# Keeping the two parts of each split weight tile in DRAM

## The chip, the cores and the metric

The kernel runs on one core of one Trainium2 chip. The metric is the device time of one launch in microseconds: the median of three runs.

## The reference

One inference step of a two-layer decoder trunk, for a prompt of 2048 tokens and a sample group of 8 sequences with one new token and 2048 past tokens each (width 1024, all in float32). Both groups share the weights.

```python
def even_mixer(x, past_kv, w_in, w_sp, b_sp):          # layer 0
    h = einsum('btd,de->bte', x, w_in)                 # 1024 x 3584
    u, v, gate_a, q, k, vb, gate_b = split(h)
    out_a = chunk_spatial_gate(gelu(u), standardize(gelu(v))) * silu(gate_a)
    out_b = stick_breaking(q, keys, vals) * silu(gate_b)
    return concat([out_a, out_b])

def odd_mixer(x, ...):                                 # layer 1
    h = einsum('btd,de->bte', x, w_in)                 # 1024 x 2468
    q, kv, q_idx, k_idx, w_idx, gate_c, p, gate_d = split(h)
    out_c = dsa_attend(top 256 keys by the index scores) * silu(gate_c)
    out_d = multiscale_pool(p) * silu(gate_d)
    return concat([out_c, out_d])

x = layer_norm(alpha * x + mixer(x) @ w_out[layer])    # 1024 x 1024, after each mixer
```

The outputs are both groups' results and the new entries of the caches.

## The kernel before, in words

The prompt is cut into four blocks of 512 tokens. For each block there is an input projection of layer 0 (`p0`, 28 weight tiles of 1024 x 128), an output projection of layer 0 (`out_proj` with `out0`, 8 weight tiles of 512 x 256), two parts of the input projection of layer 1 (`p1a`, 8 tiles, one of them only 36 columns wide; `p1b`, 12 tiles) and an output projection of layer 1 (`out1`, 8 tiles). Every block goes through the same weights, so each tile is used four times; the last block's `out1` is done in two parts, and its tail takes four of the tiles a second time (lines 1823 to 1835).

All these products are made to nearly full float32 precision on TensorE by splitting both operands in two parts of 12 bits each, hi + lo = the value, and adding three products (`proj`, lines 165 to 167; `out_proj`, lines 560 to 562). A weight tile is split anew each time it is used, in `load_w` (lines 86 to 95): a transfer brings the raw tile from the input (line 89: 512 KB, in rows of 512 B for the input projections and of 1 KB for the output projections), ScalarE casts it to hi (line 91), and GpSimd and VectorE each subtract one half for lo (line 94). The raw tiles have two buffers (tag `wr`), hi and lo two each (tags `wh`, `wl`; 4 KB of each partition per buffer). There are 260 such loads: 112 of layer 0's input weights, 80 of layer 1's and 68 of the output weights.

The order of the weights is written out as a list of stages (`plan_w`, line 243). Two tiles are loaded ahead; then each `proj` takes one tile from the list `wready` and at its end starts the load of a later one (`more_w`, line 262). `out_proj` takes two tiles at once, the two halves of the contraction for 256 columns, goes over the four token tiles in two pairs, and calls `more_w` when the last token tile of the second pair is done with a half.

The work is traced by generators. `par` (line 1837) runs several streams side by side, each at its share of an estimated cost, and the framework then orders the instructions of each engine by a simulated time line with the traced order as priority. The stages (lines 1782 to 1835) come in three contexts, each with its own pools of SBUF:

- first context: `p0(0)` alone with the sample group's columns; then `p0(1)`, `o0(0)` with `p0(2)`, and `p1a(0)`, `p1b(0)`, `o0(1)`, `p0(3)`, each beside mixer B of the block before and the sample group's attention over its cached pages (`sample0`, a third stream);
- second context: `o0(2)`, `p1a(1)`, `p1b(1)`, `p1a(2)`, `p1b(2)` beside mixer C's first tiles, with the rest of mixer B in the third stream;
- third context: `o0(3)`, `p1a(3)`, `p1b(3)` and the output projections of layer 1 beside mixer C's later tiles and the sample group's layer 1.

All ordinary transfers are issued by SyncE's one queue: raw weights, the parts of q, k and v (`qsc`, `ksc`, `vsc`), which go through DRAM and come back for each step of mixer B, the sample group's pages (`pg`), and so on. A transfer that waits for a buffer holds up those issued after it.

The functions that the change touches are these.

Of the kernel before, what the change touches and what calls it, by code (L numbers as in the profile page):

```python
# [19 lines left out]
P = 128  # L20
D = 1024
# [14 lines left out]
BUFS = {"tmp": 4, "tok": 4, "ot": 3, "hl": 1, "wr": 2}  # L36
# [18 lines left out]
class Body:  # L55
    def __init__(self, ctx, tc, I, O):
# [7 lines left out]
        self.wp = pool("wp", 2)  # L64
# [3 lines left out]
    # ---------------------------------------------------------------- helpers  # L68
# [5 lines left out]
    def split(self, hi, lo, src, heng, leng):  # L74
        """hi + lo = src exactly, hi and lo of 12 bits each"""
# [10 lines left out]
    def load_w(self, src, shape, pool, bufs=2):  # L86
        nc = self.nc
        raw = self.loc.tile(shape, F32, tag="wr", name="wr", bufs=self.bufs["wr"])
        nc.sync.dma_start(raw, src)
        hi, lo = (pool.tile(shape, F32R, tag=n, name=n, bufs=bufs) for n in ("wh", "wl"))  # L90
        nc.scalar.copy(hi, raw)  # L91
        h = shape[1] // 2
        for e, c in ((nc.gpsimd, slice(0, h)), (nc.vector, slice(h, 2 * h))):
            e.tensor_tensor(lo[:, c], raw[:, c], hi[:, c].bitcast(F32), op=OP.subtract)  # L94
        return hi, lo

    def rsqrt(self, out, var, eps, n):
        """out = (var + eps) ** -0.5, [n, k] in SBUF"""
# [14 lines left out]
    def ps(self, name, shape=(P, TB)):  # L113
        """a PSUM bank, of the first of its pools that the phase has"""
# [12 lines left out]
    # ---------------------------------------------------------------- tokens  # L127
    def load_xT(self, src, after=False, lag=0):
        """512 tokens, channels on partitions, in two parts; after: of rows that are still to be normalized"""
# [46 lines left out]
    def sample_proj(self, smp, w, m, c0):  # L176
        """the sample group's columns: [16, m] = parts of x by tokens, then summed with channels on partitions"""
# [18 lines left out]
    # ---------------------------------------------------------------- layer 0  # L196
    def setup0(self):
# [17 lines left out]
        # scratch  # L215
# [10 lines left out]
    def pools(self, bufs, navb=0, navc=0, width=0):  # L226
        """the pools of a phase; its mixer C takes tiles of up to width keys"""
# [15 lines left out]
    def plan_w(self, stages):  # L243
        """the weights that the stages take, in their order; two tiles are loaded ahead"""
        I = self.I
        self.wplan, self.wready = [], []
        for st in stages:
            if st[:3] == "out":
                w = I["w_out"][int(st[3])]
                self.wplan += [(w[hf * 512:(hf + 1) * 512, cg * 256:(cg + 1) * 256], [P, 4, 256])  # L250
                               for cg in range(4) for hf in HALVES[int(st[3])]]
                continue
# [5 lines left out]
            self.wplan += [(w[:, c:c + n], [P, KT, n]) for c, n in cols]  # L258
        for _ in range(2):
            self.more_w()  # L260

    def more_w(self, pool=None):
        if self.wplan:
            src, shape = self.wplan.pop(0)
            src = src.rearrange("(kt p) n -> p kt n", p=P)
            self.wready.append(self.load_w(src, shape, *((pool, 4) if pool else (self.wp,))))

    def gelu2(self, ps, out):
        """2 gelu(ps) to out (SBUF)"""
# [16 lines left out]
    def p0(self, i, smp=None):  # L286
        """projections of block i, mixer A, and what mixer B needs"""
# [13 lines left out]
        # q  # L301
# [7 lines left out]
        # k  # L309
# [19 lines left out]
        # v: its channels on partitions, with the token before the block in column 0  # L329
# [27 lines left out]
        # mixer A  # L357
# [14 lines left out]
        # gate of B  # L372
# [34 lines left out]
    def weave(self, a, b):  # L407
        """two generators in turns; the value of the first, which yields None while it needs the second to go on"""
# [30 lines left out]
    def b_logits(self, i, step, prev):  # L439
        """1 - sigmoid of the logits of four query tiles to one block of keys, as a product from the last key on"""  # L440
# [35 lines left out]
    def b_values(self, i, step, Ps):  # L476
        """the products, transposed, times the differences of the values"""
# [1416 lines left out]
```

## Time and profile before

| | |
|---|---|
| median of three runs | 3286.61 us (3285.94 to 3306.84) |
| profiled execution, span | 3300.5 us |
| profiled execution, mean granted clock of TensorE | 0.933 |
| TensorE busy (matmul) | 2941.0 us, 89% |
| VectorE busy | 2363.4 us, 72% |
| ScalarE busy | 1592.6 us, 48% |
| GpSimd busy | 1100.1 us, 33% |
| moved by DMA | 536.68 MB, 163 GB/s over the span |

The profile is of one execution; its own time is the span from the first to the last instruction, 3300.5 us, 13.9 us above the median of the runs. PE is TensorE's matmuls, PEld its weight loads, DVE VectorE, ACT ScalarE, POOL GpSimd, SP SyncE. A group's row gives line, engine, operation, what it writes and reads, its count, then busy microseconds and mean nanoseconds of one, then the engine's idle time just before it and who ended it. In a table of stretches come start and end, length, the busy time of each engine with its instructions in brackets, and last the granted clock as a share of full speed, the share of the 16 DMA engines that was busy, and GB/s.

### The profile page before, as it was taken

How to read it: one execution, taken by the hardware profiler on the slowest of the kernel's cores; microseconds unless marked ns; L12 is line 12 of the kernel's file. 1: busy time of each engine (PE TensorE's matmuls, PEld its weight loads, DVE VectorE, ACT ScalarE, POOL GpSimd, SP SyncE). 2: the span in 40 equal slices, each digit the busy share in tenths (PEclk: the TensorE clock that was granted, in tenths of full speed). 3: DMA queues.
4: the chain of work that ended last, by engine and by line, in shares of the span. 5: the costliest groups of instructions: out<-in, count | busy, mean ns of one | idle time of the engine just before them, and what ended most of it. 6: DMA issues, size and time to landing. Idle time of an engine off the chain costs nothing. (4 is left out here: it accounts for less than half of the span.)

```text
span 3300.5 us, 53011 instructions
## 1 busy us (share of the span) xinstructions
PE 2941.0 (89%) x17490; PEld 2339.4 (71%) x17490; DVE 2363.4 (72%) x5797; ACT 1592.6 (48%) x3212; POOL 1100.1 (33%) x1188
## 2 busy tenths in 40 slices
PE   8996999999899888998798898897979899989897
PEld 6774776777678667787576566665857778878676
DVE  2255477776876787669868988786798677697845
ACT  3332434244334233444345666565566567557653
POOL 2231334432324333242322312224322344444422
PEclk9997999999899999999799899998979999989898
DMA  7436767786575667454564344333555455657542
GB/s 224 125 108 158 235 194 217 233 239 177 173 220 151 205 207 227 144 169 120 158 172 114 111 132 127 98 92 91 154 175 140 131 170 160 196 171 211 181 130 66
DMA packets 543391, 536.68 MB, mean 163 GB/s; under 512 B 43831, under 2 KB 408528, under 8 KB 543079
## 3 DMA queue, kind: packets, MB, share of 16 engines
q1 hardware_dynamic: 533231, 497.39, 51.9%
q0 software_dynamic: 9856, 35.66, 3.5%
q8 instruction: 139, 2.28, 0.3%
q14 instruction: 165, 1.35, 0.1%
HBM read 439.19 MB, written 93.92 MB: 162 GB/s over the span
## 5 line engine op out<-in xcount | busy, mean ns | idle before, releaser
L94 POOL TENSOR_TENSOR wl<-wr,wh 128x512 fp32r<-128x512 f32 x260 | 413.4, 1591 | 945.0 <-ACT wh L91 844.8
L165 PE MATMUL pp<-xh,wh 128*128 128x512 f32 x1536 | 625.2, 412 | 18.7 <-DVE q_hl L84 5.3
L166 PE MATMUL pp<-xl,wh 128*128 128x512 f32 x1536 | 621.5, 405 | 14.6 <-DVE xl L84 9.8
L167 PE MATMUL pp<-xh,wl 128*128 128x512 f32 x1536 | 618.3, 403 | 1.9 <-POOL wl L94 1.9
L91 ACT CAST wh<-wr 128x1024 fp32r<-128x1024 f32 x260 | 269.9, 1039 | 338.7 <-PE pp L166 135.3
L471 DVE TENSOR_TENSOR_SCAN P<-P 128x512 f32<-128x512 f32 (+2 forms) x320 | 380.3, 1201 | 53.9 <-ACT P L464 25.3
L165 PEld LDWEIGHTS pp<-xh,wh 128*128 128x128 f32 x1536 | 293.3, 192 | 96.2 <-issue 11.4
L166 PEld LDWEIGHTS pp<-xl,wh 128*128 128x128 f32 x1536 | 294.1, 192 | 74.6 <-DVE xl L84 16.2
L94 DVE TENSOR_TENSOR wl<-wr,wh 128x512 fp32r<-128x512 f32 x260 | 226.8, 873 | 163.3 <-ACT wh L91 154.3
L167 PEld LDWEIGHTS pp<-xh,wl 128*128 128x128 f32 x1536 | 293.2, 191 | 65.3 <-POOL wl L94 4.4
L560 PE MATMUL pp_o<-wh,oh 128*128 128x256 f32 x1008 | 297.1, 299 | 18.9 <-DVE xres L565 9.1
L561 PE MATMUL pp_o<-wl,oh 128*128 128x256 f32 x1008 | 292.5, 293 | 1.2 <-POOL wl L94 1.1
L562 PE MATMUL pp_o<-wh,ol 128*128 128x256 f32 x1008 | 288.8, 294 | 0.9 <-POOL ol L84 0.7
L1194 PE MATMUL z_c<-ksc,qc 128*128 128x512 f32 (+3 forms) x816 | 226.4, 370 | 48.9 <-DVE mx L1196 41.6
L1212 ACT ACTIVATE zt<-zt,nmax 128x512 f32<-128x512 f32 (+3 forms) x320 | 207.4, 651 | 118.9 <-DVE nmax L1200 118.7
L1181 POOL TENSOR_TENSOR nm<-nm,mk 128x256 f32<-128x256 f32 (+1 forms) x128 | 95.0, 743 | 449.6 <-DMA nm<-bft 293.3
L78 ACT CAST ph<-ps_p 128x512 fp32r<-128x512 f32 (+1 forms) x320 | 164.5, 524 | 165.9 <-PE ps_p L490 156.5
L84 DVE TENSOR_TENSOR pl<-ps_p,ph 128x512 fp32r<-128x512 f32 (+1 forms) x320 | 189.4, 598 | 74.4 <-ACT ph L78 73.7
L457 PE MATMUL z<-ks,q 128*128 128x512 f32 (+3 forms) x640 | 199.3, 402 | 38.3 <-DVE mx L1196 23.4
L1239 PE MATMUL av_c<-zt,vsc 128*64 128x128 f32 x2176 | 216.9, 301 | 16.5 <-ACT zt L1227 16.3
L1227 ACT COPY zt<-ps_pc 128x512 f32<-128x512 f32 (+3 forms) x320 | 162.8, 518 | 135.1 <-PE ps_pc L1225 131.6
L940 ACT ACTIVATE mk<-ix,tk_tn 128x384 int8<-128x384 f32 (+13 forms) x140 | 183.5, 1310 | 86.5 <-DVE tk_tn L990 46.2
(460 smaller groups left out, 6311.0 us busy)
## 6 DMA issues: line engine op xcount, KB each, us to landing
pg<-cache_b_kv SPq DMA_DIRECT2D x256, 256.0 KB
wr<-w_in_even SPq DMA_DIRECT2D x112, 512.0 KB
wr<-w_in_odd SPq DMA_DIRECT2D x76, 512.0 KB
wr<-w_out SPq DMA_DIRECT2D x68, 512.0 KB
ks<-ksc SPq DMA_DIRECT2D x80, 256.0 KB
vs<-vsc SPq DMA_DIRECT2D x80, 256.0 KB
ksc<-kcs SPq DMA_DIRECT2D x80, 256.0 KB
q<-qsc SPq DMA_DIRECT2D x64, 256.0 KB
```

Of the source, the lines that this page charges most:

```text
L91: nc.scalar.copy(hi, raw)
L94: e.tensor_tensor(lo[:, c], raw[:, c], hi[:, c].bitcast(F32), op=OP.subtract)
L165: nc.tensor.matmul(ps[:m], wh[:, kt, :m], xh[kt], start=a, stop=False)
L166: nc.tensor.matmul(ps[:m], wh[:, kt, :m], xl[kt], start=False, stop=False)
L167: nc.tensor.matmul(ps[:m], wl[:, kt, :m], xh[kt], start=False, stop=b)
L471: nc.vector.tensor_tensor_scan(r, r, r, initial=ini, op0=OP.mult, op1=OP.bypass)
L560: nc.tensor.matmul(ps[:, :256], oh[:, tt], wh[:, k], start=a, stop=False)
L561: nc.tensor.matmul(ps[:, :256], oh[:, tt], wl[:, k], start=False, stop=False)
L562: nc.tensor.matmul(ps[:, :256], ol[:, tt], wh[:, k], start=False, stop=b)
L1194: nc.tensor.matmul(z[:, :n], q2[:, c, jj % 2, :].bitcast(F32R), kk, start=c == 0, stop=c == 1)
L1212: nc.scalar.activation(zt, zt, AF.Exp, bias=nmx, accum_out=st["rs"][:, h, c:c + 1])
L1239: nc.tensor.matmul(self.av[64 * a:64 * a + 64, g, jj // 2, :], vs[:, k, :], pT[:, k * P:(k + 1) * P], start=kb == 0, stop=kb == nkb - 1)
```

## The change

A weight tile's two parts now lie side by side in one tile `w2` (8 KB of each partition, three buffers). The first time a tile is used it is loaded raw and split as before, and then both parts are written to a scratch tensor in DRAM, 1 MB, 8 KB in a row for each partition. Each later use reads this tensor back in one transfer straight into `w2`, with no cast and no subtraction. A key (stage and column, or layer, column group and half) tells whether a tile has been kept.

The raw tiles' two buffers are in a pool of the first context alone. So that layer 1's output weights, whose first use is later, are split by then too, `split_ahead(1)` takes its 8 tiles through split and write at the end of the third stream of the first context's last stage. There are 64 different tiles; so 64 raw loads with their splits, 64 writes and 204 reads take the place of 260 raw loads with their splits.

```diff
-BUFS = {"tmp": 4, "tok": 4, "ot": 3, "hl": 1, "wr": 2}
+BUFS = {"tmp": 4, "tok": 4, "ot": 3, "hl": 1}
...
-        self.wp = pool("wp", 2)
+        self.wp = pool("wp", 3)
+        self.wkept = {}
...
-    def load_w(self, src, shape, pool, bufs=2):
+    def load_w(self, key, src, shape, pool, bufs):
         nc = self.nc
-        raw = self.loc.tile(shape, F32, tag="wr", name="wr", bufs=self.bufs["wr"])
+        w2 = pool.tile([P, 2, shape[1] * shape[2]], F32R, tag="w2", name="w2", bufs=bufs)
+        hi, lo = (w2[:, c].rearrange("p (k n) -> p k n", k=shape[1]) for c in range(2))
+        if key in self.wkept:
+            nc.sync.dma_start(w2.bitcast(F32), self.wkept[key])
+            return hi, lo
+        raw = self.wraw.tile(shape, F32, tag="wr", name="wr", bufs=2)
         nc.sync.dma_start(raw, src)
-        hi, lo = (pool.tile(shape, F32R, tag=n, name=n, bufs=bufs) for n in ("wh", "wl"))
         nc.scalar.copy(hi, raw)
         h = shape[1] // 2
         for e, c in ((nc.gpsimd, slice(0, h)), (nc.vector, slice(h, 2 * h))):
             e.tensor_tensor(lo[:, c], raw[:, c], hi[:, c].bitcast(F32), op=OP.subtract)
+        d = self.wkept[key] = self.dr.tile([P, 2, shape[1] * shape[2]], F32, name=f"wk{len(self.wkept)}")
+        nc.sync.dma_start(d, w2.bitcast(F32))
         return hi, lo
...
-            self.wplan += [(w[:, c:c + n], [P, KT, n]) for c, n in cols]
+            self.wplan += [((st[:2], c), w[:, c:c + n], [P, KT, n]) for c, n in cols]
...
+    def out_w(self, layer):
+        w = self.I["w_out"][layer]
+        return [((f"out{layer}", cg, hf), w[hf * 512:(hf + 1) * 512, cg * 256:(cg + 1) * 256], [P, 4, 256])
+                for cg in range(4) for hf in HALVES[layer]]
+
+    def take_w(self, key, src, shape, pool, bufs):
+        return self.load_w(key, src.rearrange("(kt p) n -> p kt n", p=P), shape, pool, bufs)
+
     def more_w(self, pool=None):
         if self.wplan:
-            src, shape = self.wplan.pop(0)
-            src = src.rearrange("(kt p) n -> p kt n", p=P)
-            self.wready.append(self.load_w(src, shape, *((pool, 4) if pool else (self.wp,))))
+            self.wready.append(self.take_w(*self.wplan.pop(0), pool or self.wp, 4 if pool else 3))
+
+    def split_ahead(self, layer):
+        for w in self.out_w(layer):
+            self.take_w(*w, self.wp, 3)
+            yield 1.0
...
             self.pools(BUFS_A, navb=1)
+            self.wraw = self.cx.enter_context(self.tc.tile_pool(name="wraw", bufs=2))
...
-            self.par([(p1a(0), PB), (p1b(0), PC), (o0(1), PO), (p0(3), PA)], [(mb(2), B(2))], [(until(bg, 1000), S0[2])], early=EARLY[0])
+            self.par([(p1a(0), PB), (p1b(0), PC), (o0(1), PO), (p0(3), PA)], [(mb(2), B(2))], [(until(bg, 1000), S0[2]), (self.split_ahead(1), 8)], early=EARLY[0])
```

More of the change, by code (lines that the diff above doesn't have):

```diff
@@ L248, in plan_w @@
             if st[:3] == "out":
-                w = I["w_out"][int(st[3])]
-                self.wplan += [(w[hf * 512:(hf + 1) * 512, cg * 256:(cg + 1) * 256], [P, 4, 256])
-                               for cg in range(4) for hf in HALVES[int(st[3])]]
+                self.wplan += self.out_w(int(st[3]))
                 continue
```

## The prediction

> **What bounds the kernel now.** I read the page's busy times first, then the span cut into the three phases that the code has (0 to 300 us: block 0 alone; 300 to 1450 us: layer 0 beside mixer B and the sample group; 1450 to 3300 us: mostly layer 1), and then the idle time of TensorE (PE).
>
> ```profile
> span 3300.5 us, 53011 instructions
> PE 2941.0 (89%) x17490; PEld 2339.4 (71%) x17490; DVE 2363.4 (72%) x5797; ACT 1592.6 (48%) x3212; POOL 1100.1 (33%) x1188
> DMA packets 543391, 536.68 MB, mean 163 GB/s; under 512 B 43831, under 2 KB 408528, under 8 KB 543079
> ```
>
> ```profile
> 0.00:300.00 300.00, 251.12 (x1458) 202.18 (x1459) 103.61 (x268) 92.59 (x179) 71.14 (x70) 0.93 0.52 142
> 300.00:1450.00 1150.00, 1066.53 (x5338) 821.46 (x5336) 816.00 (x1280) 437.09 (x824) 395.32 (x423) 0.96 0.67 202
> 1450.00:3300.00 1850.00, 1623.38 (x10696) 1315.76 (x10696) 1443.76 (x4250) 1062.97 (x2211) 633.62 (x697) 0.92 0.49 142
> ```
>
> The columns after the length are PE, PEld, DVE, ACT and POOL busy, then the granted clock of PE, the share of the 16 DMA engines and GB/s. PE is the bound with 89%, but not a full one: it idles 83.5 us in the middle phase (1150 - 1066.5) and 226.6 us in the late one (1850 - 1623.4), and where it idles its clock is lower too: 0.96 and 0.92. At 0.92 the late phase's 1623 us hold some 130 us of lost speed, so beside each idle microsecond stands 0.57 us of slow clock (130 / 226.6); in the middle phase 0.04 x 1066.5 / 83.5 = 0.51.
>
> What ends PE's idle time are above all answers of VectorE (DVE), not weights (us in total, times, longest):
>
> ```profile
> PE z_c L1194 <- DVE mx L1196: 41.6, 29, 6.5
> PE av L497 <- DVE pl L84: 24.9, 20, 7.4
> PE z L457 <- DVE mx L1196: 23.4, 15, 3.3
> PE ps_sav L1417 <- DMA pg<-cache_b_kv: 5.0, 6, 1.4
> PE pp L167 <- POOL wl L94: 1.9, 3, 1.1
> ```
>
> The only wait of a projection for its split weights is 1.9 us in the whole span. So the split is hidden, and removing it can help PE only through the engines that it loads.
>
> **What the change removes.**
>
> ```profile
> L94 POOL TENSOR_TENSOR wl<-wr,wh 128x512 fp32r<-128x512 f32 x260 | 413.4, 1591 | 945.0 <-ACT wh L91 844.8
> L91 ACT CAST wh<-wr 128x1024 fp32r<-128x1024 f32 x260 | 269.9, 1039 | 338.7 <-PE pp L166 135.3
> L94 DVE TENSOR_TENSOR wl<-wr,wh 128x512 fp32r<-128x512 f32 x260 | 226.8, 873 | 163.3 <-ACT wh L91 154.3
> 300.00:1450.00 1150.00, 98.72 (x118) 195.76 (x119) 0.96 0.67 202
> 1450.00:3300.00 1850.00, 101.10 (x110) 163.00 (x111) 0.92 0.49 142
> ```
>
> (The last two rows are line 94 alone, DVE and POOL.) There are 64 different tiles: 28 of `p0`, 20 of `p1a` and `p1b`, 8 of each output projection. So 260 - 64 = 196 splits go: 196 x 1.039 = 204 us of ACT, 196 x 1.591 = 312 us of POOL, 196 x 0.873 = 171 us of DVE. By phase: the late one loses all of its 110 (DVE 101.1 us, 7% of its 1443.8). The middle one has 36 left instead of 118 (8 of `out0`, 20 of `p1`, and the 8 of `out1` that `split_ahead` moves there), so 82 x 0.837 = 69 us of its DVE go.
>
> **What that is worth.** If PE were the only bound, nothing; if DVE were, all 170 us. I count it where DVE is at its end, in the stretches of 100 us in which DVE is over 83% busy and PE under 90% (of these 800 to 900 us is left out, since it holds first splits, which stay). First all engines, then line 94 alone:
>
> ```profile
> 1100.00:1200.00 100.00, 86.33 (x530) 69.47 (x528) 83.32 (x136) 26.42 (x46) 32.92 (x39) 0.93 0.63 182
> 1500.00:1600.00 100.00, 73.99 (x421) 55.94 (x419) 89.74 (x259) 37.59 (x91) 30.02 (x37) 0.80 0.45 130
> 1800.00:1900.00 100.00, 79.04 (x391) 56.99 (x390) 90.80 (x285) 60.39 (x138) 37.24 (x50) 0.81 0.40 113
> 2100.00:2200.00 100.00, 89.02 (x531) 68.32 (x529) 88.14 (x248) 66.70 (x140) 30.46 (x39) 0.94 0.38 100
> 2400.00:2500.00 100.00, 81.11 (x458) 61.33 (x459) 94.55 (x299) 67.38 (x137) 30.73 (x37) 0.83 0.53 160
> 2900.00:3000.00 100.00, 88.23 (x659) 75.63 (x656) 88.87 (x244) 61.54 (x121) 44.85 (x38) 0.90 0.62 197
> ```
>
> ```profile
> 1100.00:1200.00 100.00, 8.38 (x8) 12.65 (x8) 0.93 0.63 182
> 1500.00:1600.00 100.00, 4.07 (x5) 7.63 (x5) 0.80 0.45 130
> 1800.00:1900.00 100.00, 0.99 (x2) 1.80 (x2) 0.81 0.40 113
> 2100.00:2200.00 100.00, 5.38 (x5) 7.71 (x5) 0.94 0.38 100
> 2400.00:2500.00 100.00, 3.38 (x5) 6.61 (x5) 0.83 0.53 160
> 2900.00:3000.00 100.00, 4.17 (x4) 5.16 (x4) 0.90 0.62 197
> ```
>
> The late five hold 17.99 us, with the clock that comes back 17.99 x 1.57 = **-28.2 us**; 1100 to 1200 us holds 8.38 x 1.51 = **-12.7 us**. The bounds of this term are 0 and all of it, 101.1 + 69 = 170 us. I stay near the low end, since where most splits stand PE has no room: 300 to 400 us (row below) has 12 and PE at 95%.
>
> ACT's and POOL's freed time I cost at nothing: ACT is busy 57% of the late phase and POOL 34%. Next to be late there is DVE itself (`mx`, line 1196), which stays.
>
> **What the change adds: transfers.** 196 raw loads of 512 KB go, of which four are only 144 KB (the 36-column tile: 3 of these go), -101.6 MB; 204 reads of 1 MB come (84 `p0`, 60 `p1`, 24 `out0`, 36 `out1`), +211.7 MB; 64 writes, +66.4 MB. Together 536.7 + 176.5 = 713 MB. In the first phase the 28 writes add 29.4 MB to 142 GB/s x 300 us, 240 GB/s, under the 252 GB/s that the kernel already reaches in one stretch of the middle phase, so nothing. The late phase gets about 57 MB on 263 MB, at its own rate (142 / 0.49 = 290 GB/s) a share of 0.60: nothing. The middle phase gets 84 x 0.524 for `p0`, 8 x 1.05 + 8 x 0.524 for `out0`, 20.2 for `p1`'s writes and 8 x 1.57 for `split_ahead`: 89.4 MB on 232 MB. At its own rate, 202 / 0.67 = 301 GB/s, its share goes from 0.67 to 0.93. In its fullest stretches that is about all there is (all engines, then line 94 alone, which counts the tiles):
>
> ```profile
> 300.00:400.00 100.00, 94.98 (x438) 71.74 (x436) 59.19 (x103) 36.74 (x72) 33.92 (x46) 0.97 0.82 243
> 1200.00:1300.00 100.00, 97.74 (x452) 70.60 (x451) 69.94 (x100) 42.47 (x73) 24.25 (x20) 0.98 0.79 252
> ```
>
> ```profile
> 300.00:400.00 100.00, 11.22 (x12) 19.58 (x13) 0.97 0.82 243
> 1200.00:1300.00 100.00, 9.55 (x10) 17.96 (x11) 0.98 0.79 252
> ```
>
> 300 to 400 us has 12 tiles, + 6.3 MB at 296 GB/s, 0.82 + 0.21 = 1.03; 1200 to 1300 us, 10 tiles at 319 GB/s, 0.95 without what `split_ahead` may bring there. These sums take the mean rate of today's packets, of which three quarters are under 2 KB; kept tiles have 8 KB in a row on both sides, so the truth may lie lower. The Trainium skill's page "DMA: Bandwidth & Descriptors", Specifications, gives 435 GB/s for all 16 engines; by that figure the middle phase would stand at 0.85, an estimate that no row here shows.
>
> Is a read in time? With empty queues the first raw load was issued at 0.8 us and its cast began at 4.8 us (first and last start):
>
> ```profile
> L89 SPq DMA_DIRECT2D wr<-w_in_even x112: 367/388/1508, 0.8 to 1426.8; - x112
> L91 ACT CAST wh<-wr x260: 420/1048/1092, 4.8 to 3232.5; 128x1024 fp32r<-128x1024 f32 x126, 128x288 fp32r<-128x288 f32 x4
> L165 PE MATMUL pp<-xh,wh x59: 387/393/497, 451.2 to 499.7; 128*128 128x512 f32 x59
> L560 PE MATMUL pp_o<-wh,oh x128: 274/283/415, 1447.4 to 1546.0; 128*128 128x256 f32 x128
> ```
>
> So 4.0 us for half a megabyte, and 5.6 to 5.8 us for a whole one at 290 to 319 GB/s. A projection tile takes 8 of line 165, 6.7 us at its fastest (48.5 us / 7.25 tiles), and with three slots a read has two tiles, 13.4 us. An output projection uses two slots at once for a column group of 25 us (98.6 / 4); the slot for the next group's second tile is freed at three quarters of this group and needed at the first quarter of the next, 12 us. Both hold with a factor of two, which a middle phase at 0.93 may eat. PE waits for DMA there little today, the most for the cache pages, 5.0 us; I take twice that, 10 us, with 0 as the lower end and the third rival below as the upper.
>
> `split_ahead` takes the third slot 8 times: cast 1.05, subtraction 1.6, write 3.5 us or more, some 6.2 us, one tile's time. Its lower bound is 0, its upper 8 x 6.7 = 54; since one tile still lies ready, I take 5 us.
>
> Behind what does it queue? SyncE (SP) issues all of these transfers in the written order:
>
> ```profile
> SPq L89 <- DVE wl L94: 425.6, 155, 14.9
> SPq L89 <- POOL wl L94: 103.0, 91, 5.5
> ```
>
> SP stands 528.6 us before raw loads today, waiting for the split that frees a raw slot. After, a read waits for PE instead, and the 64 writes wait for DVE and POOL; behind them wait `ks`, `vs`, `q` and the cache pages. More or less than today cannot be read here; I take it as equal, and its ends are the far terms of the rivals.
>
> **The sum:** -28.2 - 12.7 + 10 + 5 = -26 us, 3274.5 us of span. The profiled execution is 0.4% over the median of the runs, so in proportion 3274.5 / 3300.5 x 3286.61 = **3261 us**.
>
> **Rivals.**
>
> *Relief hidden.* PE's waits are chains (matmul, DVE, matmul) and not a lack of DVE time; in 300 to 400 us DVE is at 59% and PE at 95% all the same. Then only the 15 us or less of cost stay: 3287 to 3302, say 3294 us.
>
> *Relief in full.* DVE is the pace of all of the late phase: -101.1 - 12.7 + 15 = -99 us, 3188 us. For it speaks that DVE's durations spread wherever POOL works:
>
> ```profile
> L94 DVE TENSOR_TENSOR wl<-wr,wh x260: 294/693/2241, 5.9 to 3233.6; 128x512 fp32r<-128x512 f32 x126, 128x144 fp32r<-128x144 f32 x4
> L471 DVE TENSOR_TENSOR_SCAN P<-P x320: 386/1268/8372, 242.5 to 2261.6; 128x512 f32<-128x512 f32 x96, 128x128 f32<-128x128 f32 x32, 128x384 f32<-128x384 f32 x32
> ```
>
> With 312 us fewer of POOL such long ones would be fewer. The Trainium skill states this as a rule ("SBUF — State Buffer", Who interferes with whom): a DVE instruction with two SBUF inputs and a GpSimd one that reads SBUF shut each other out for a whole instruction. By that rule, the spread agrees. Against it: 97.7% of PE at 1200 to 1300 us.
>
> *Reads late in the middle phase (slower).* From the point where the DMA engines are full, between 300 and 1450 us, the 92 reads there land after PE wants them. Gain and loss are even at (40.9 - 5) / (92 x 1.51) = 0.26 us of lateness each. At half a microsecond it is 92 x 0.5 x 1.51 = 70 us, 12.7 us of relief don't come, the late relief stays: 70 + 5 - 28.2 = +47, 3333 us; at 1 us 3402 us. For it: 0.82 + 0.21 in one stretch; against it: 8 KB rows, and a spare of two tiles. The Trainium skill speaks against the change here ("TensorE: Matmul & The Clock Gate", HAM oscillation): a wait for weights past some 3.4 us halves the clock each time. The 0.80 beside 74% of PE at 1500 to 1600 us agrees; the 1.51 has it in.
>
> *No reuse.* The keys name layer, column and half, the same for each block, so this can be left out.
>
> **Chances.** My case (3227 to 3282, that is -60 to -5 us) 0.44; hidden 0.15; in full 0.12; late reads 0.29. One per cent, about what a measurement of this kernel can tell from no change, is 33 us: below 3254 lie 0.21 of my case and the full relief, 0.33; slower than 3319 0.28; within 0.39. The range of 3200 to 3350 leaves out some 0.08 below and 0.1 above.
>
> **What would show it.** 64 casts of line 91's kind instead of 260, the last before 1450 us; DVE 171 us less busy; 713 MB; fewer `z_c <- mx` waits after 1450 us, clock over 0.92 there. Wrong would be: waits of `pp` or `pp_o` for a DMA of the weights beyond 10 us, a middle phase longer than today's with a DMA share near 1, or a late phase that keeps its length although DVE has its 101 us less.

## The result, and the profile after

The changed kernel takes 3326.27 us (median of 4 runs, 3315.99 to 3331.23), the kernel before, run beside it, 3289.61 us (4 runs, 3285.94 to 3306.84). The ratio is 1.0105 with a 95% interval of 1.0082 to 1.0127: slower by a good one per cent, where 3261 us had been forecast.

The page of the kernel after, its busy times and its transfers:

```profile
span 3323.6 us, 52238 instructions
PE 2944.1 (89%) x17490; PEld 2341.4 (70%) x17490; DVE 2162.0 (65%) x5601; ACT 1418.1 (43%) x3016; POOL 789.4 (24%) x992
DMA packets 404759, 712.99 MB, mean 215 GB/s; under 512 B 41911, under 2 KB 235600, under 8 KB 370663
```

All that the change takes away is away. VectorE is busy 201 us less than before (2363.4 - 2162.0), ScalarE 174 us, GpSimd 311 us, and the bytes are the 713 MB worked out. The span is longer all the same. The same three stretches as in the prediction, all engines:

```profile
0.00:300.00 300.00, 238.58 (x1373) 192.62 (x1373) 97.80 (x250) 82.09 (x160) 65.75 (x65) 0.93 0.80 240
300.00:1450.00 1150.00, 1060.26 (x5290) 812.30 (x5291) 734.16 (x1199) 365.40 (x743) 245.02 (x334) 0.95 0.83 275
1450.00:3300.00 1850.00, 1640.38 (x10792) 1332.05 (x10790) 1315.41 (x4105) 970.17 (x2112) 473.07 (x589) 0.93 0.55 174
```

The first has the 240 GB/s that was expected, but the engines' share has gone from 0.52 to 0.80, and PE does 238.6 us of work in it in place of 251.1. The middle one reaches 0.83, not full, and PE does 1060.3 us in place of 1066.5, though VectorE has 82 us less to do there.

Stretches of fixed bounds hold different work in the two kernels. Two marks are the same piece of work in both: the last of the 224 first-kind matmuls of `p0(0)` (28 tiles of 8), and the first and last scores of mixer C (`z_c`). The line of a group gives its first and its last start. Kernel before:

```profile
L165 PE MATMUL pp<-xh,wh x224: 387/389/797, 14.7 to 236.0; 128*128 128x512 f32 x112
L1194 PE MATMUL z_c<-ksc,qc x816: 220/384/799, 1462.5 to 3260.5; 128*128 128x512 f32 x65, 128*128 128x256 f32 x58, 128*128 128x128 f32 x35, 128*128 128x384 f32 x6
```

Kernel after:

```profile
L173 PE MATMUL pp<-xh,w x224: 387/389/797, 16.5 to 254.0; 128*128 128x512 f32 x112
L1212 PE MATMUL z_c<-ksc,qc x816: 220/384/796, 1500.0 to 3285.0; 128*128 128x512 f32 x65, 128*128 128x256 f32 x58, 128*128 128x128 f32 x35, 128*128 128x384 f32 x6
```

This gives three lengths that are used for all kernels below: block 0 (to the first mark) 236.0 before and 254.0 after, **+18.0 us**; the middle (from there to the first `z_c`) 1226.5 and 1246.0, **+19.5 us**; the late phase (first to last `z_c`) 1798.0 and 1785.0, **-13.0 us**. So there is a gain, and it is where it was looked for; the first 1500 us lose three times as much. The three add up to +24.5 us, while the medians differ by 36.7: the profiled execution of the kernel before was a long one (a span of 3300.5 us), so its lengths may be some us too long.

Block 0 loses most of its time in the first 100 us. There PE is busy 11.8 us less than before; the first row is the kernel before, the second the one after:

```profile
0.00:100.00 100.00, 83.67 (x474) 66.66 (x475) 26.15 (x70) 29.54 (x51) 23.47 (x32) 0.98 0.74 209
0.00:100.00 100.00, 71.89 (x399) 57.02 (x400) 26.10 (x60) 25.07 (x43) 19.43 (x30) 0.95 0.93 284
```

In steps of 25 us, before:

```profile
25.00:50.00 25.00, 22.73 (x148) 18.10 (x147) 5.78 (x10) 5.89 (x11) 5.37 (x3) 1.00 0.93 283
50.00:75.00 25.00, 23.53 (x135) 19.05 (x133) 5.25 (x10) 8.18 (x14) 5.39 (x3) 0.93 0.65 191
75.00:100.00 25.00, 25.00 (x139) 20.13 (x137) 5.42 (x14) 7.39 (x13) 6.42 (x4) 1.00 0.53 141
```

and after:

```profile
25.00:50.00 25.00, 19.18 (x102) 14.74 (x101) 7.17 (x9) 5.84 (x10) 2.99 (x2) 0.86 0.94 291
50.00:75.00 25.00, 20.72 (x132) 16.90 (x130) 4.69 (x9) 4.29 (x8) 3.08 (x2) 0.93 1.05 336
75.00:100.00 25.00, 21.78 (x131) 17.71 (x130) 4.43 (x8) 7.53 (x13) 5.35 (x3) 1.00 0.81 253
```

From 25 to 50 us the transfers of the start already took 0.93 of the engines before; the writes of the first tiles come on top, and PE idles 13.3 us in these 75 us in place of 3.7.

The chain of waits of PE after has a new head (us in total, times, longest), and two that are smaller than before (41.6 and 23.4 us):

```profile
PE pp L173 <- DMA w<-wk: 32.2, 16, 8.7
PE z_c L1212 <- DVE mx L1214: 31.1, 23, 3.9
PE z L475 <- DVE mx L1214: 9.9, 9, 2.3
PE pp_o L578 <- DMA w<-wk: 3.6, 3, 1.8
```

Of the first group, this lies between 300 and 1450 us:

```profile
PE pp L173 <- DMA w<-wk: 15.0, 4, 8.7
```

SyncE's queue stands before the reads (line 93) for a slot that PE still uses, and before the writes (line 102) for the subtractions. Some of the groups:

```profile
SPq L93 <- PE pp L175: 143.4, 51, 10.0
SPq L102 <- DVE w L100: 89.2, 35, 11.0
SPq L93 <- PE pp_o L580: 78.3, 27, 12.6
SPq L102 <- POOL w L100: 27.2, 28, 1.1
```

### The profile page after: what moved, and what is told of

It reads as the page before. It is cut to its first block, busy times and chain, and to the rows that moved or that the text cites. A ratio compares the mean times of both kernels' runs of the same rounds, so it can differ in the third digit from the quotient of the medians.

```text
span 3323.6 us, 52238 instructions
## 1 busy us (share of the span) xinstructions
PE 2944.1 (89%) x17490; PEld 2341.4 (70%) x17490; DVE 2162.0 (65%) x5601; ACT 1418.1 (43%) x3016; POOL 789.4 (24%) x992
## 5 line engine op out<-in xcount | busy, mean ns | idle before, releaser
L173 PE MATMUL pp<-xh,w 128*128 128x512 f32 x1536 | 632.6, 418 | 62.7 <-DMA w<-wk 32.2
L174 PE MATMUL pp<-xl,w 128*128 128x512 f32 x1536 | 628.9, 409 | 5.7 <-DVE xl L85 5.7
L175 PE MATMUL pp<-xh,w 128*128 128x512 f32 x1536 | 623.7, 406 | 0.0
L489 DVE TENSOR_TENSOR_SCAN P<-P 128x512 f32<-128x512 f32 (+2 forms) x320 | 362.8, 1145 | 85.1 <-POOL P L485 47.1
L173 PEld LDWEIGHTS pp<-xh,w 128*128 128x128 f32 x1536 | 297.0, 195 | 147.1 <-DMA w<-wk 34.4
L174 PEld LDWEIGHTS pp<-xl,w 128*128 128x128 f32 x1536 | 298.8, 195 | 68.9 <-DVE xl L85 9.1
L175 PEld LDWEIGHTS pp<-xh,w 128*128 128x128 f32 x1536 | 297.7, 194 | 64.0 <-issue 2.9
L578 PE MATMUL pp_o<-w,oh 128*128 128x256 f32 x1008 | 297.9, 298 | 24.7 <-DVE xres L583 12.1
L579 PE MATMUL pp_o<-w,oh 128*128 128x256 f32 x1008 | 289.3, 289 | 0.0
L580 PE MATMUL pp_o<-w,ol 128*128 128x256 f32 x1008 | 288.0, 292 | 1.0 <-POOL ol L85 0.8
L79 ACT CAST ph<-ps_p 128x512 fp32r<-128x512 f32 (+1 forms) x320 | 165.4, 524 | 260.4 <-PE ps_p L508 235.5
L1212 PE MATMUL z_c<-ksc,qc 128*128 128x512 f32 (+3 forms) x816 | 223.1, 364 | 36.2 <-DVE mx L1214 31.1
L578 PEld LDWEIGHTS pp_o<-w,oh 128*128 128x128 f32 x1008 | 195.3, 194 | 40.8 <-DVE xres L583 14.9
L1214 DVE CUSTOM_DVE_ANT_0 zt<-z_c,mk 128x512 f32<-128x512 f32 (+3 forms) x256 | 148.7, 588 | 102.3 <-PE z_c L1212 63.0
L1243 PE MATMUL ps_pc<-idf,zt 128*128 128x128 f32 x1088 | 192.5, 296 | 19.8 <-DVE hT L200 7.2
```

The lines of the kernel that those rows point to most:

```text
L173: nc.tensor.matmul(ps[:m], wh[:, kt, :m], xh[kt], start=a, stop=False)
L174: nc.tensor.matmul(ps[:m], wh[:, kt, :m], xl[kt], start=False, stop=False)
L175: nc.tensor.matmul(ps[:m], wl[:, kt, :m], xh[kt], start=False, stop=b)
L489: nc.vector.tensor_tensor_scan(r, r, r, initial=ini, op0=OP.mult, op1=OP.bypass)
L578: nc.tensor.matmul(ps[:, :256], oh[:, tt], wh[:, k], start=a, stop=False)
L579: nc.tensor.matmul(ps[:, :256], oh[:, tt], wl[:, k], start=False, stop=False)
```

## The experiments

The theory after the result: the relief of the split engines is real and about of the size forecast, and the added transfers cost more than it, in block 0 and in the middle. The rivals: there is no relief; or the reads are merely late, each as one large transfer; or the number of transfers and their waits on SyncE's queue cost the time, not their bytes. Five rounds each; "ratio" is to the kernel before on the same chip. All edits are to the changed kernel unless another is named.

**1. The writes of block 0.** Two ways to take `p0`'s 28 tiles out: never keep them (e1), or keep them when they are split for the second time (e2).

```diff
+        if key[0] == "p0":                       # e1
+            return hi, lo
         d = self.wkept[key] = self.dr.tile(...)
```
```diff
+        if key[0] == "p0" and key not in self.wseen:     # e2
+            self.wseen.add(key)
+            return hi, lo
         d = self.wkept[key] = self.dr.tile(...)
```

> The tiles of p0 are never kept: all four blocks load them raw and split them; the output projections and layer 1 stay as in the changed kernel (36 writes, 120 reads). Theory A (the transfers of p0's kept tiles made the loss: its 28 writes in the first 300 us, its 84 reads in the middle phase, and the relief of the split engines is worth nothing): 3288 to 3302 us. Rival B (the relief is real, some 26 us, and all added transfers together cost 60): with p0's transfers gone and the late relief kept, about 3275 us. Rival C (any change of the order moves this kernel by one per cent, whatever it does): anywhere between 3255 and 3330 us.

> The tiles of p0 are kept only at their second use, in block 1: the 28 writes move out of the first 300 us, and block 1 splits instead of reading. Theory A: the 17 us that the changed kernel is behind at the end of block 0 are gone, block 1 then has the writes beside full DMA engines: 3300 to 3318 us, and block 0 ends within 3 us of the kernel before. Rival B: 3310 us as well. If the first phase's loss comes from the order and not from the writes, block 0 ends late all the same.

Measured: e1 3283.24 us, ratio 0.9977 [0.9963, 0.9992]; e2 3308.59 us, 1.0062 [1.0041, 1.0082]. The lengths of block 0, middle and late phase are 235.5, 1238.9, 1774.3 us in e1 and 236, 1259, 1762 us in e2. Without its writes block 0 is back at the 236 us of before, so the 18 us there are theirs. In e2 the 28 writes, and 56 reads, stand in the middle phase, and that grows by 20 us against e1. Both keep a late phase 24 and 36 us shorter than before. The time of e2 lies where both theories had it, that of e1 between the two. Kernel e1 is the one version with both parts of the weights that comes out ahead of both kernels, by a quarter of a per cent, which is no more than e3 below moves without any change of the work; it still has all its reads in layer 1 and the output projections. First e1, then e2:

```profile
L175 PE MATMUL pp<-xh,w x224: 387/389/793, 17.1 to 235.5; 128*128 128x512 f32 x112
L1214 PE MATMUL z_c<-ksc,qc x816: 220/385/796, 1474.4 to 3248.7; 128*128 128x512 f32 x65, 128*128 128x256 f32 x58, 128*128 128x128 f32 x35, 128*128 128x384 f32 x6
L176 PE MATMUL pp<-xh,w x224: 387/389/796, 17.6 to 235.8; 128*128 128x512 f32 x112
L1215 PE MATMUL z_c<-ksc,qc x816: 220/384/796, 1494.8 to 3256.9; 128*128 128x512 f32 x65, 128*128 128x256 f32 x58, 128*128 128x128 f32 x35, 128*128 128x384 f32 x6
```

**2. The common tile alone.** The kernel before, with hi and lo in one tile as the change has them, nothing kept.

```diff
-        hi, lo = (pool.tile(shape, F32R, tag=n, name=n, bufs=bufs) for n in ("wh", "wl"))
+        w2 = pool.tile([P, 2, shape[1] * shape[2]], F32R, tag="w2", name="w2", bufs=bufs)
+        hi, lo = (w2[:, c].rearrange("p (k n) -> p k n", k=shape[1]) for c in range(2))
```

> The kernel before, with hi and lo side by side in one tile (two slots), nothing kept: a control for the layout and for what a mere change of tiles does. Theory A and rival B: 3283 to 3297 us, as before. Rival C: more than 10 us away from before.

Measured: 3296.87 us, ratio 1.0023 [1.0008, 1.0038]; 234.2, 1218.1, 1797.8 us. The same work comes out 7 us later by the medians and 10 us earlier by the profiled execution (a span of 3290.1 against 3300.5 us). Two things blur a comparison by that much: the framework orders the engines' instructions anew for any change, and a profiled execution is one sample (that of the kernel before is 11 us above its median of 3289.61). So a difference of some 10 us in a stretch is no evidence by itself.

**3. The relief without half of the traffic.** The second part is a tile of zeros that lies in SBUF: 64 casts, no subtraction, and writes and reads of 512 KB.

```diff
-        w2 = pool.tile([P, 2, shape[1] * shape[2]], F32R, tag="w2", name="w2", bufs=bufs)
-        hi, lo = (w2[:, c].rearrange(...) for c in range(2))
+        w2 = pool.tile([P, n], F32R, tag="w2", name="w2", bufs=bufs)
+        hi, lo = (x.rearrange(...) for x in (w2, self.wzero[:, :n]))
...
-        for e, c in ((nc.gpsimd, slice(0, h)), (nc.vector, slice(h, 2 * h))):
-            e.tensor_tensor(lo[:, c], raw[:, c], hi[:, c].bitcast(F32), op=OP.subtract)
```

> The changed kernel with the second part of the weights left out of the computation (lo is a tile of zeros): 64 casts, no subtraction at all, writes and reads of 512 KB, so about the bytes of the kernel before and 33 MB of writes. Theory A (relief worth nothing, cost goes with the bytes): 3293 to 3308 us, block 0 some 8 us behind, the late phase (from the first output projection of block 2's attention at about 1450 us) as long as in both kernels, 1800 to 1812 us. Rival B (relief real): 3255 to 3275 us, the late phase under 1785 us.

Measured: 3380.79 us, ratio 1.028 [1.0255, 1.0306]. This does not speak of the transfers. With weights of one part the index scores change, and the branch that selects the top keys exactly was taken; PE stood there once for 153.5 us, a wait that no other kernel here shows:

```profile
PE ps_sl L1692 <- ACT s_tmp L1688: 153.7, 2, 153.5
```

So e5 is e4 with that branch never taken (a row that would need it keeps a wrong mask):

```diff
-        with self.tc.If(rv > 0):
+        with self.tc.If(rv > P - 1):
```

> The kernel of e4 (second part of the weights left out, 512 KB per read and write), and the slow exact selection, into which e4's other numbers sent one tile for 155 us, is held shut, as it stays in the kernel before (so a row that would need it keeps a wrong mask). Theory D (the relief of the split engines is worth 55 to 75 us, and the added bytes cost that and more): e4 less 155 us, 3215 to 3235 us. Theory A (relief worth nothing): 3285 to 3305 us.

Measured: 3231.56 us, ratio 0.9824 [0.9812, 0.9837]; 250.5, 1191.5, 1755.7 us:

```profile
L174 PE MATMUL pp<-xh,w x224: 388/397/794, 15.8 to 250.5; 128*128 128x512 f32 x112
L1213 PE MATMUL z_c<-ksc,qc x816: 218/387/940, 1442.0 to 3197.7; 128*128 128x512 f32 x65, 128*128 128x256 f32 x58, 128*128 128x128 f32 x35, 128*128 128x384 f32 x6
300.00:1450.00 1150.00, 1092.44 (x5583) 839.58 (x5584) 720.16 (x1212) 381.05 (x780) 204.37 (x323) 0.98 0.72 226
```

Without the splits, and with half of the traffic for the kept tiles, the middle is 35.0 us and the late phase 42.3 us shorter than before. The rival without a relief falls. This kernel also lacks the 64 first splits' subtractions, and a third of its weight products are with zeros; what both are worth is bounded below (e13).

**4. Second reads: too much in one step.** To e5, behind each of its 204 reads a second one into a tile that nobody uses: a full one (e6), one of 64 KB (e9), and full ones for `p0` alone (e10) and for all but `p0` (e11).

```diff
             nc.sync.dma_start(w2.bitcast(F32), self.wkept[key])
+            more = pool.tile([P, n], F32, tag="more", name="more", bufs=2)
+            nc.sync.dma_start(more, self.wkept[key])             # e6
+            nc.sync.dma_start(more[:, :n // 8], self.wkept[key][:, :n // 8])     # e9, in its place
```

> As e5, and each of the 204 reads is followed by a second one of the same 512 KB into a tile that nobody uses: the bytes read of the changed kernel, but TensorE waits only for the first half. Theory D1 (the traffic itself costs: full DMA engines delay everything): e5 plus 40 to 90 us, 3260 to 3320 us. Theory D2 (the cost is that a tile of 1 MB lands later than one of 512 KB, right before TensorE wants it): within 15 us of e5.

> As the run with a second read behind each of the 204 reads, but the second read brings only an eighth of the tile (64 KB in place of 512 KB): as many transfers on SyncE's queue, 13 MB more in place of 107. If the bytes cost the 59 us between the one-read run (ratio 0.9824) and the two-read run (1.0004), this one stays within 12 us of the one-read run: 3232 to 3244 us, ratio 0.982 to 0.986. If the number of transfers costs it (their issue and their place in the queue), it comes out near the two-read run: 3275 to 3290 us, ratio 0.996 to 1.0004. Like those two it leaves out the second part of the weights and holds the exact selection shut.

> The full second read only behind the 84 reads of p0, nearly all of them between 230 and 1450 us, 44 MB. If traffic costs where the DMA engines are already busy (0.72 in the middle phase of the one-read run, 0.47 in the late one), most of the 59 us comes back: 3231.6 + 40 to 48 = 3272 to 3280 us, ratio 0.994 to 0.998. If each second read costs the same wherever it stands, 84 / 204 x 59 = 24 us: 3256 us, ratio 0.9896. It leaves out the second part of the weights and holds the exact selection shut.

> The full second read only behind the other 120 reads (p1a, p1b, out0, out1), nearly all after 1000 us, 63 MB. If traffic costs where the DMA engines are already busy: 11 to 19 us, 3243 to 3251 us, ratio 0.986 to 0.988. If each second read costs the same wherever it stands, 120 / 204 x 59 = 35 us: 3266 us, ratio 0.993. It leaves out the second part of the weights and holds the exact selection shut.

Measured:

| kernel | us | ratio | block 0, middle, late phase, us |
|---|---|---|---|
| e6, 204 second reads of 512 KB | 3290.33 | 1.0004 [0.9987, 1.0021] | 259.6, 1231.2, 1757.4 |
| e9, 204 of 64 KB | 3301.01 | 1.0031 [1.0017, 1.0046] | 252.0, 1236.3, 1773.2 |
| e10, 84 of 512 KB (`p0`) | 3272.81 | 0.9944 [0.9926, 0.9962] | 258, 1209, 1765 |
| e11, 120 of 512 KB (the rest) | 3281.59 | 0.9963 [0.9946, 0.9980] | 250, 1219, 1782 |

By e6 alone the bytes would have been the cause: +59 us. e9 takes that reading away: an eighth of the bytes costs at least as much, and 41 us (e10) and 50 us (e11) do not add up to 59. The waits of SyncE's queue in e9 show what the second reads did besides:

```profile
SPq L99 <- DMA more<-wk: 82.2, 77, 4.9
SPq L99 <- DMA wk<-w: 72.8, 35, 3.9
```

The order put many of them right behind the write of the same tile (the first at 13.9 us, long before the first use), and there the queue stood 155 us until an earlier transfer had landed, with everything else behind it. Issuing them took the queue another 204 x 0.32 = 65 us, while its waits of all kinds together are no longer than in e5 (about 2030 against 2060 us). So the second reads cost time almost without bytes; whether by these waits, by the issuing or by the new order is not separated, and these four runs cannot say what the bytes cost.

**5. The bytes without another transfer.** To e5 again: each read brings 1 MB in one transfer, the kept half twice, into a tile of the changed kernel's size (e12); and the 64 writes are of 1 MB too (e13). The second half is never used. e13 has every transfer of the changed kernel, and none of its subtractions. In both the zeros of the second part come from one column of a small tile.

```diff
-        w2 = pool.tile([P, n], F32R, tag="w2", name="w2", bufs=bufs)
+        w2 = pool.tile([P, 2, n], F32R, tag="w2", name="w2", bufs=bufs)
...
-            nc.sync.dma_start(w2.bitcast(F32), self.wkept[key])
+            nc.sync.dma_start(w2.bitcast(F32), self.wkept[key].unsqueeze(1).to_broadcast([P, 2, n]))     # e12
+            nc.sync.dma_start(w2.bitcast(F32), self.wkept[key])        # e13, wkept being [P, 2, n]
...
-        nc.sync.dma_start(d, w2.bitcast(F32))
+        nc.sync.dma_start(d, w2[:, 0].bitcast(F32))                                    # e12
+        nc.sync.dma_start(d, w2[:, :1].bitcast(F32).to_broadcast([P, 2, n]))           # e13
```

> As the one-read run (ratio 0.9824, which leaves out the second part of the weights and holds the exact selection shut), but each of the 204 reads brings 1 MB in one transfer, as in the changed kernel; its second half is not used. So the bytes come back without one more transfer on SyncE's queue. If the bytes of the reads cost time: 3231.6 + 40 to 60 us, ratio 0.994 to 1.001. If it was the second transfer and its waits on SyncE that cost the time of the two-read runs: 0.982 to 0.987.

> As the run before, and the 64 writes are of 1 MB too: all transfers of the changed kernel, none of its 128 subtractions. Bytes theory: another 10 to 20 us, lost in block 0, ratio 0.999 to 1.006; the rest to 1.0105 is then the first splits' subtractions and the writes' waits for them. Queue theory: 0.983 to 0.989, and the changed kernel's loss is in the waits of the writes for the subtractions. It leaves out the second part of the weights and holds the exact selection shut.

Measured: e12 3273.26 us, ratio 0.9950 [0.9934, 0.9966]; e13 3316.28 us, 1.0092 [1.0071, 1.0114]. The lines of e12:

```profile
L174 PE MATMUL pp<-xh,w x224: 387/393/796, 15.7 to 249.2; 128*128 128x512 f32 x112
L1213 PE MATMUL z_c<-ksc,qc x816: 218/386/1202, 1474.1 to 3232.2; 128*128 128x512 f32 x65, 128*128 128x256 f32 x58, 128*128 128x128 f32 x35, 128*128 128x384 f32 x6
300.00:1450.00 1150.00, 1071.61 (x5408) 820.42 (x5407) 704.29 (x1170) 369.96 (x753) 191.51 (x307) 0.97 0.80 263
```

and of e13:

```profile
L174 PE MATMUL pp<-xh,w x224: 387/394/797, 18.5 to 259.2; 128*128 128x512 f32 x112
L1213 PE MATMUL z_c<-ksc,qc x816: 218/386/1095, 1499.7 to 3278.5; 128*128 128x512 f32 x65, 128*128 128x256 f32 x58, 128*128 128x128 f32 x35, 128*128 128x384 f32 x6
300.00:1450.00 1150.00, 1072.98 (x5312) 807.48 (x5312) 702.35 (x1164) 365.61 (x744) 190.65 (x299) 0.97 0.83 275
```

The steps from the kernel before to the one after, by the marks (differences of the lengths above, one execution each, to be read to 10 us, in the late phase to 20, as is seen below):

| step | block 0 | middle | late |
|---|---|---|---|
| before to e5: no re-splits, no subtractions, half of the kept tiles' traffic | +14.5 | -35.0 | -42.3 |
| e5 to e12: reads of 1 MB for 512 KB | -1.3 | **+33.4** | +2.4 |
| e12 to e13: writes of 1 MB for 512 KB | **+10.0** | **+15.6** | +20.7 |
| e13 to after: the 64 tiles' subtractions, and real second parts | -5.2 | +5.5 | +6.2 |
| together | +18.0 | +19.5 | -13.0 |

By the medians the same steps are -58 us to e5 (3231.56 against 3289.61), +42 us to e12, +43 us to e13 and +10 us to the kernel after. The two steps that only add bytes are six times what e3 moved without any change of the work, so the bytes do it, in the main: in the middle the second halves of reads and writes cost 49 us and take all of the relief there, at a share that went from 0.72 to 0.83. The step to e13 is more than twice the 10 to 20 us expected. A read of e12 has twice the packets of one of e5, a read of e13 has not (404,756 packets in all in e5, 430,870 in e12, 412,949 in e13), and the middle is no shorter in e13; so it is not the number of packets. The same reads cost nothing that can be told in the late phase (+2.4 us), where the engines' share is 0.55. The kernel with all transfers and none of the subtractions has a ratio of 1.0092 against the changed kernel's 1.0105, so the first splits' subtractions are not the loss, and products with zeros do not make e5 fast. The waits of the queue before the writes stay in it (107.0 us for ScalarE, 120.9 us in the changed kernel, 117.4 us in e5); they do not tell these kernels apart.

How the bytes reach PE, in the middle phase from mark to mark (e5, e12, e13), and PE's waits of a projection for its weights in the whole span of the same three:

```profile
250.50:1442.00 1191.50, 1105.64 (x5628) 847.48 (x5627) 731.20 (x1272) 384.44 (x789) 211.81 (x331) 0.97 0.72 221
249.20:1474.10 1224.90, 1111.79 (x5640) 854.05 (x5639) 733.38 (x1272) 384.08 (x789) 207.68 (x331) 0.96 0.79 256
259.20:1499.70 1240.50, 1134.67 (x5650) 858.97 (x5649) 738.14 (x1273) 386.36 (x790) 217.11 (x331) 0.96 0.82 268
```

```profile
PE pp L174 <- DMA w<-wk: 14.6, 13, 2.9
PE pp L174 <- DMA w<-wk: 13.8, 14, 2.0
PE pp L174 <- DMA w<-wk: 19.7, 15, 3.6
```

From e5 to e12 PE idles 27 us more (113.1 against 85.9) and the waits for weights do not grow. From e12 to e13 it idles less, and its matmuls are busy 23 us longer at the same granted clock (some 2 us of it for the ten more that are counted), which no row here explains.

Another term isn't explained either: the +20.7 us of the late phase from e12 to e13, where no tile is written any more. The late lengths of the kernels with one-part weights go from 1755.7 (e5) over 1757.4 (e6, with second reads there) to 1782 us (e11), not in the order of their traffic; since each of these kernels has its own order of instructions, I take this for the order's doing, but no run isolates it.

**6. Lateness, and the queue.** Each read cut in two halves along the contraction, so that the first matmuls have theirs sooner (e7), the same on e1 (e8); and each kept tile written at the next tile's load, so that its subtractions have time to end (e14), the same on e1 (e15).

```diff
-            nc.sync.dma_start(w2.bitcast(F32), self.wkept[key])        # e7, e8
+            h = shape[1] * shape[2] // 2
+            for c in (slice(0, h), slice(h, 2 * h)):
+                nc.sync.dma_start(w2[:, :, c].bitcast(F32), self.wkept[key][:, :, c])
```
```diff
+        while self.wlate:                                              # e14, e15
+            nc.sync.dma_start(*self.wlate.pop())
         w2 = pool.tile([P, 2, shape[1] * shape[2]], F32R, tag="w2", name="w2", bufs=bufs)
...
-        nc.sync.dma_start(d, w2.bitcast(F32))
+        self.wlate.append((d, w2.bitcast(F32)))
```

> The changed kernel with each read cut in two of 512 KB, first and second half of the contraction, so that the first products can begin when half has landed. D1: 3320 to 3335 us, as the changed kernel. D2: the waits for w<-wk (36 us on the whole, half a read each) go: 3290 to 3312 us.

> Both: p0 never kept (as e1, 3283 us), reads cut in two. D1: 3278 to 3290 us. D2: 3265 to 3278 us, a version faster than both kernels.

> The changed kernel, with each kept tile written at the next tile's load, when its subtractions are done; SyncE waited 116 us for them before the writes. If that waiting of the queue costs the time: ratio 1.000 to 1.004 in place of 1.0105. If the traffic costs it: 1.008 to 1.013.

> The kernel that keeps all but p0 (0.9977), with each kept tile written at the next tile's load. Its writes waited 35 us for the subtractions: if that costs time 0.990 to 0.995, otherwise 0.996 to 1.000.

Measured: e7 3332.96 us, ratio 1.0128 [1.0113, 1.0142]; e8 3309.53 us, 1.0072 [1.0059, 1.0085]; e14 3310.31 us, 1.0074 [1.0053, 1.0095]; e15 3288.43 us, 0.9993 [0.9977, 1.0009]. Cutting the reads doesn't help; on e1 it costs 26 us (3309.53 - 3283.24), the same bytes in more transfers, which agrees with e9. Since more transfers cost time of their own, this cannot show that landing sooner is worth nothing; that late reads are not the main cause is seen in e12, where the middle grows by 33 us and the waits for weights do not. Writing later has a ratio 0.003 below the changed kernel's, with intervals that overlap, and lies between the two forecasts; on e1 it gains nothing. But the edit does not take the waits away that it was made to take away. The queue stands before the writes of e14 as long as before those of the changed kernel (89.2 and 27.2 us):

```profile
SPq L92 <- DVE w L103: 91.9, 32, 9.7
SPq L92 <- POOL w L103: 30.0, 30, 1.1
```

In e15 it is 34.6 us against 36.2 in e1. So what these waits cost, in block 0 above all, stays open.

## Why the prediction was wrong

**What goes, and the bytes: right.** 64 casts, VectorE 201 us less (171 were counted for the split; the rest comes from other operations that take less time at the same count, the scans of line 471 for one, 380.3 us before and 362.8 after), GpSimd 311 us against 312, ScalarE 174 against 204, 713 MB.

**By phase.** The sum had 0 for block 0, -12.7 + 10 + 5 = +2.3 us for the middle and -28.2 for the late phase. The marks show +18.0, +19.5 and -13.0. The signs named as showing the change right came, too: 64 casts, the last at 1427.6 us; 713 MB; fewer `z_c` waits for `mx`; a clock of 0.93 in the late phase. They show that the work is gone, not what the transfers cost.

**The relief: right in kind, and not far off in size.** -28.2 us were taken for the late phase. It measures -13.0 in the changed kernel, -24 in e1, -36 in e2 and -42 in e5 (with all transfers, e13, -19), so the step holds to within what the order of instructions moves. For the middle -12.7 us were taken; e5 shows -35.0, without the first splits' subtractions and with half of the traffic. I had counted only the stretches with VectorE above 83% and PE below 90%; there is relief outside of these. The rival of a hidden relief falls with e5, that of a full one (-99 us) with e5's -42 us in the late phase.

**"In the first phase ... so nothing": the first step that failed.** The 240 GB/s came true to the digit, and the writes cost 18.0 us. I had compared a mean over 300 us with a stretch of 252 GB/s elsewhere. The start is not even: before, the engines stood at 0.93 from 25 to 50 us and at 0.53 from 75 to 100 us, and the writes of the first tiles fall into the full part. e1 and e2 show that it is these writes, since block 0 is back at 236 us without them. The loss is not in proportion to their bytes: with half of the bytes per write (e5) block 0 is already 14.5 us longer, and in no run is a write taken out without the queue's wait before it, so bytes and waits are not separated there.

**+10 us for the transfers of the middle phase: the second step that failed, and the largest.** The share of 0.93 was too high (0.83; the rate per full share is 275 / 0.83 = 331 GB/s against 301), and yet the cost was sized too low: 49 us for the second halves of the kept tiles in e12 and e13 together. I asked only whether a read lands before its tile is wanted. The traffic isn't felt there alone: in the changed kernel's whole span 35.8 us of PE's waits name the weights (32.2 + 3.6), 15.0 us of them in the middle, while in e12 and e13 such waits of `pp` are only 13.8 and 19.7 us against 14.6 in e5. The other transfers of that phase (the parts of q, k and v that go through DRAM, the pages) use the same queue. Through what the rest reaches PE isn't settled: from e5 to e13 the middle has 20 us more of idle time, in many short waits, and 29 us more of busy PE.

**Late phase at a share of 0.60, nothing: right.** It is 0.55, and doubling the reads' bytes there costs 2.4 us, to be read to some 20.

**`split_ahead` +5 us: not tried alone. SyncE "equal": right in the sum.** With all groups of these lines added, the queue stands about 547 us before the raw loads in the kernel before, and in the changed one about 549 us: 426.0 before the reads, 120.9 before the writes, 1.8 before the raw loads. So the queue does not wait longer as a whole; that the two sums agree so closely is luck, since one waits for splits and the other mostly for PE. What its waits cost where they now stand is not separated.

**The rival "reads late in the middle phase"** has the right sign and place, and its 3333 us lies near the 3326 measured; that is luck, since its mechanism is a part at most. It needed full engines and reads that are late each by half a microsecond. The engines are not full over the phase (0.83), the late reads there are four waits of 15.0 us together, it had no loss in block 0, and the clock, which that rival had falling with each wait, is 0.95 in the middle against 0.96. The Trainium skill's rule on waits for weights past 3.4 us ("TensorE: Matmul & The Clock Gate", HAM oscillation) can act here in 16 waits at most, of 8.7 us the longest; the granted clock gives it a small part. Of the three signs named as wrong, one came whole: waits of `pp` and `pp_o` for the weights' DMA beyond 10 us. Of the second, the middle is longer, but at a share of 0.83 and not near 1; the third, a late phase of the same length, did not come.

**Readings of the profile before.** The list of PE's waits left out the second largest group:

```profile
PE ps_x L141 <- DMA xc<-x_prompt: 27.4, 4, 24.4
PE ps_x L149 <- DMA xc<-x_prompt: 31.6, 4, 25.4
```

The second row is the kernel after. One wait of about 25 us for an input's transfer stands in every kernel here, so it is not the loss; but it shows that PE did wait for a DMA before. And the 1.9 us were not the only wait for split weights: the output projections had 1.8 us more (`pp_o`, 1.1 for the second part and 0.7 for the first).

## What to carry to other kernels

Price added traffic stretch by stretch, against what the DMA engines already do there: here half a megabyte more per read cost nothing that could be told at a share of 0.55, and 33 us for the 95 reads issued there (0.35 us each) where it lifted the share from 0.72 to 0.80, before the engines were full and without showing as a wait for the tile that was read. Give the first 100 us a row of their own; a mean over the first phase hides that the start is full. To test a saving against its traffic, change the bytes of a transfer and not the number of transfers: another transfer on a shared queue brings costs of its own (e9), and a read in two parts can cost more than it hastens (e8). And look in the trace whether an edit took away the wait that it was made for: e14 and e15 did not.

## What was not expected of the hardware

A stretch of 25 us with the DMA engines at their fullest, 1.05 in the record, moved 336 GB/s, and the one before it 291 GB/s at 0.94: both come to 310 to 320 GB/s for a full share. The 435 GB/s of the Trainium skill's page "DMA: Bandwidth & Descriptors", Specifications, which the prediction had also weighed, is given there as a ceiling; no stretch shown here comes near it.

The same page (Issuing engines are not separate DMA queues) says that the time a sequencer takes to issue a transfer is usually small beside the transfer. The 0.32 us of each issue here agree for a read of 1 MB, which at 331 GB/s is an estimated 3.2 us; but 204 small second reads, 13 MB, made the kernel 69 us longer than e5 (3301.01 - 3231.56), with 65 us more of issuing on the one queue and 155 us of its waits for earlier transfers in front of them.
